# State space scan: running sums spread over the partitions by transfers, one subtraction per step, weight sums three loads behind

## The chip, the cores and the metric

The kernel runs on one core of a Trainium2 chip. The metric is the device time of one execution in microseconds (us). A core has a matrix engine, TensorE (PE), with its weight loader (PEld), three elementwise engines, VectorE (DVE), ScalarE (ACT) and GpSimd (POOL), SyncE (SP), which here only issues transfers, and 16 DMA engines that move data between the device memory and the on-chip memory SBUF. Products land in PSUM, a second on-chip memory of eight banks.

## What is computed

The reference is a decoder trunk of two layers for 1024 tokens of width 1024. Layer 0 has a state space part and a gated short convolution side by side; layer 1 has attention over a sliding window. Each is followed by a norm, a gated feed-forward part and a gate of its own. The change touches the state space part and some sums that a later norm needs. The state space part has 16 heads of 64 channels in two groups and works in chunks of 128 tokens:

```python
a_cs = jnp.cumsum(da, axis=2)
seg = a_cs[:, :, :, None] - a_cs[:, :, None, :]
decay_ls = jnp.exp(jnp.where(causal, seg, -jnp.inf))
cb = jnp.einsum('bclgn,bcsgn->bclsg', cm, bm)
y_diag = jnp.einsum('bclsgr,bcsgrp->bclgrp', cb[..., None] * decay_ls, xdt)
...
y_off = jnp.einsum('bclgn,bcgrpn->bclgrp', cm, h_in) * jnp.exp(a_cs)[..., None]
y = y_diag + y_off + xs * d_skip
```

`a_cs` is the running sum of a head's decays within a chunk. For each head and chunk, a 128 x 128 mask holds the exponential of the difference of two of its values, for every pair of tokens.

## The kernel before

Activations lie with features on the partitions and tokens along the row. The large products are of fp32 numbers that are split in a high and a low part, so that one tile takes three products (L134, L135, L136). A weight unit of 128 x 1024 comes by `unit()` (L118 to L131): SP issues the load of `st` (L128), ACT rounds it to the high part (L129), and DVE or POOL makes the low part (L130, on POOL alone while the scan and the short convolution run). There are two `st` buffers and three of weights. The order of the instructions on each engine is set by a scheduler from the program and from priorities, of which the units have a high one; so products that belong to later columns stand between the instructions of the scan.

`steps()` (L813 to L890) makes the decays of all heads. `acs` has the running sums with tokens on the partitions. `A2` has them with heads on the partitions and tokens along the row, as a rounded value on partitions 0 to 15 (L888) and the rest on 32 to 47 (L889). `SEL`, a table of ones and zeros that is loaded (L825) and cast, picks heads out of `A2` in a product.

`ssd(g)` (L911 to L986) is the scan of head group g. It runs over Q = 0 to 3, quarters of 256 tokens, and in each over p = 0 to 3, pairs of heads. A quarter begins with the work per chunk: transposes `xst` (L925), `xdt` (L930), the products `cb` (L932) with their causal mask `cbm` (L933), `xw`, `bt`, `btok` and the states `st` and `h` (L936 to L949). Then a step for each pair, 32 in all for both groups:

- two products with `SEL` (L957) put the running sums of the two heads on all 128 partitions, in a PSUM bank (`seg`);
- four instructions on DVE (L964), one per head and chunk, subtract the partition's own running sum and take the minimum with 0, into `m`;
- ACT takes the exponential (L966), DVE multiplies by `cbm` (L967);
- four products make `yd` (L972), up to two make `yo` (L978), and a third product with `SEL` (L980) puts the running sums beside `yo`, by channel;
- ACT takes their exponential `e` (L982), and three DVE instructions join all to y (L145, L985, L986).

The convolution of the columns x, B and C that precedes the scan takes, per half of a column, one ACT instruction (L902), three multiply-adds on DVE, a Tanh on ACT (L907) and one more on DVE; L145 is the line of a helper that all of these multiply-adds share.

Behind the scan come eight columns of the short convolution, three times 24 products for each half of the tokens. The first of the three is copied by ACT as `c` (L1034). Between them runs `centres()` (L1005 to L1020): 44 loads of 512 KB into `dc`, issued by POOL (L1013) into a pool of two buffers, and for each a sum on ACT (L1017) one load behind.

Of the kernel before, what the change touches and what calls it, by code (L numbers as in the profile page):

```python
# [7 lines left out]
F32 = mybir.dt.float32  # L8
F32R = mybir.dt.float32r
AF = mybir.ActivationFunctionType  # L10
ALU = mybir.AluOpType
# [31 lines left out]
def trunk(ctx: ExitStack, tc: tile.TileContext, xT, pT, w_in, w_dt, w_out, w_q, w_k, w_v, w_o, w_gate, w_up, w_down,  # L43
# [25 lines left out]
    def pool(stack, name, bufs=1, side=None):  # L69
        return stack.enter_context(tc.tile_pool(name=name, bufs=bufs, side=side, reuse_waits="tile"))  # L70

    def bank(tag, name):
        if "ps8" in room:
            return room["ps8"][1].tile([P, HB], F32, tag="ps", name=name, bufs=8)
        return room["ps"][1].tile([P, HB], F32, tag=tag, name=name, bufs={"g": 2, "c": 1, "a": 3, "b": 2}[tag])
# [19 lines left out]
    def hs(H):  # L95
        return slice(H * HB, (H + 1) * HB)

    def f4(pool, name, tag="f"):
        return (pool or room["r"][1]).tile([P, NT], F32, tag=tag, name=name)
# [695 lines left out]
    with ExitStack() as mctx:  # L795
# [10 lines left out]

        cwh = ts.tile([P, 60], F32, name="cwh")
        V.tensor_scalar_mul(out=cwh, in0=vec[:, VC["conv_w"]:VC["conv_w"] + 60], scalar1=0.5)
        SEL = ts.tile([P, 8, P], F32R, name="SEL")
        A2 = ts.tile([P, NT], F32R, name="A2")  # L810
        V.memset(A2[:48].bitcast(F32), 0.0)

        def steps():  # L813

            nc.sync.dma_start(cst, consts)
            A.activation(mean, ones, AF.Copy, scale=1.0 / 1024.0)
            A.activation(mean_r, ones, AF.Copy, scale=1.0 / 512.0)
            nc.sync.dma_start(row, rows.broadcast_to([P, NROW]))
            wst = ts.tile([P, KT, 16], F32, name="wst")
            nc.sync.dma_start(wst, w_dt)  # L820
            Wdt = ts.tile([P, KT, 32], F32R, name="Wdt")
            A.copy(Wdt[:, :, 0:16], wst)
            G.tensor_sub(Wdt[:, :, 16:32], wst, Wdt[:, :, 0:16].bitcast(F32))
            sst = f4(prep, "pre").rearrange("p (a b) -> p a b", b=P)
            nc.sync.dma_start(sst[:48], sel)  # L825
            A.copy(SEL[:48], sst[:48])
            dtT = [ts.tile([32, HB], F32, name="dtT", tag="h", bufs=3) for _ in range(2)]
            for H in range(2):
                ps = gps("dt")
                for i in range(KT):  # L830
                    T.matmul(ps[:32], Wdt[:, i, :], X[i][H][:, 0, :], start=i == 0, stop=False)
                    T.matmul(ps[:16], Wdt[:, i, 0:16], X[i][H][:, 1, :], start=False, stop=i == KT - 1)
                A.copy(dtT[H], ps[:32])
            dps = bank("b", "dtt")
            for c in range(NCH):
                T.transpose(dps[:, c * 32:(c + 1) * 32], dtT[c // 4][:, (c % 4) * P:(c % 4 + 1) * P], ident[:32, :32])

            def sm(name):
                return ts.tile([P, P], F32, name=name)

            def smt(name):
                return ts.tile([P, P], F32, tag="smt", name=name, bufs=4)

            def c16(ap):
                return ap.rearrange("p (c h) -> p c h", h=16)

            def b16(ap):
                return ap.unsqueeze(1).broadcast_to([P, 8, 16])

            dt, acs, dx, cd = sm("dt"), sm("acs"), sm("dx"), sm("cd")  # L850
            xr = smt("xr")
            dv = dps[:, :256].rearrange("p (c l h) -> p c l h", l=2, h=16)
            V.tensor_tensor(out=c16(xr), in0=dv[:, :, 0, :], in1=b16(row[:, 0:16]), op=ALU.add)
            V.tensor_tensor(out=c16(xr), in0=c16(xr), in1=dv[:, :, 1, :], op=ALU.add)
            e = smt("e")
            stt(e, xr, -1.0, xr, ALU.mult, ALU.max)
            A.activation(e, e, AF.Exp, scale=-1.0)
            sden = smt("sden")
            V.tensor_scalar_add(out=sden, in0=e, scalar1=2.0)
            V.reciprocal(out=sden, in_=sden)  # L860
            V.tensor_tensor(out=e, in0=e, in1=sden, op=ALU.mult)
            V.tensor_tensor(out=sden, in0=e, in1=e, op=ALU.mult)
            pol = smt("pol")
            V.tensor_scalar_mul(out=pol, in0=sden, scalar1=1.0 / 17.0)
            for k in (15, 13, 11, 9, 7, 5, 3):
                stt(pol, pol, 1.0 / k, sden, ALU.add, ALU.mult)
            stt(pol, pol, 1.0, e, ALU.add, ALU.mult)
            V.tensor_scalar_max(out=xr, in0=xr, scalar1=0.0)
            stt(dt, pol, 2.0, xr, ALU.mult, ALU.add)
            ea = ts.tile([P, 16], F32, name="ea")  # L870
            A.activation(ea, row[:, 16:32], AF.Exp)
            da = smt("da")
            stt(c16(da), c16(dt), -1.0, b16(ea), ALU.mult, ALU.mult)
            cps = bank("a", "acs")
            T.matmul(cps[:, :P], tri, da, start=True, stop=True)
            V.tensor_copy(acs, cps[:, :P])
            tps = bank("a", "tot")
            T.matmul(tps[:, :P], ones, da, start=True, stop=True)
            A.activation(cd, tps[:, :P], AF.Exp)
            V.tensor_tensor(out=dx, in0=tps[:, :P], in1=acs, op=ALU.subtract)  # L880
            A.activation(dx, dx, AF.Exp)
            V.tensor_tensor(out=dx, in0=dx, in1=dt, op=ALU.mult)
            for H in range(2):
                ps = bank("a", "acst")
                for cc in range(4):
                    c = 4 * H + cc
                    T.matmul(ps[:16, cc * P:(cc + 1) * P], da[:, c * 16:(c + 1) * 16], tri, start=True, stop=True)
                A.copy(A2[0:16, hs(H)], ps[:16])  # L888
                V.tensor_sub(A2[32:48, hs(H)], ps[:16], A2[0:16, hs(H)].bitcast(F32))  # L889
            return dt, acs, dx, cd  # L890

        BC = {}
# [18 lines left out]
        def ssd(g):  # L911
# [3 lines left out]
            for Q in range(4):  # L915
# [35 lines left out]
                qs = slice(Q * 256, (Q + 1) * 256)  # L951
                for p in range(4):
                    j = 4 * g + p
                    gp = bank("a", "seg")
                    for k in range(2):
                        hd = 8 * g + 2 * p + k
                        T.matmul(gp[:, k * 256:(k + 1) * 256], SEL[:48, j, 64 * k:64 * k + 1].broadcast_to([48, P]), A2[:48, qs],  # L957
                                 start=True, stop=True)
                    M = ts.tile([P, HB], F32, tag="m", name="m", bufs=3)
                    for k in range(2):  # L960
                        for ci in range(2):
                            a = (2 * Q + ci) * 16 + 8 * g + 2 * p + k
                            o = slice(k * 256 + ci * P, k * 256 + (ci + 1) * P)
                            V.tensor_scalar(out=M[:, o], in0=gp[:, o], scalar1=acs[:, a:a + 1], scalar2=0.0,  # L964
                                            op0=ALU.subtract, op1=ALU.min)
                    A.activation(M, M, AF.Exp)  # L966
                    V.tensor_tensor(out=M.rearrange("p (k q) -> p k q", k=2), in0=M.rearrange("p (k q) -> p k q", k=2),  # L967
                                    in1=cbm.rearrange("p c l -> p (c l)").unsqueeze(1).broadcast_to([P, 2, 256]), op=ALU.mult)
                    yd = bank("a", "yd")
# [6 lines left out]
                    for ci in range(2):  # L976
                        if hin[ci] is not None:
                            T.matmul(yo[:, ci * P:(ci + 1) * P], hin[ci][:, p * P:(p + 1) * P],  # L978
                                     Ct_[:, (2 * Q + ci) * P:(2 * Q + ci + 1) * P], start=True, stop=True)
                    T.matmul(yo[:, 256:512], SEL[:48, j, :], A2[:48, qs], start=True, stop=True)  # L980
                    e2 = ts.tile([P, 256], F32, tag="e2", name="e2", bufs=2)
                    A.activation(e2, yo[:, 256:512], AF.Exp)  # L982
                    y = YS[j][:, qs]
                    stt(y, y, vcol("ssd_d", j), yd[:, 0:256], ALU.mult, ALU.add)
                    V.tensor_tensor(out=e2[:, lo:], in0=e2[:, lo:], in1=yo[:, lo:256], op=ALU.mult)  # L985
# [17 lines left out]
        cctx = ExitStack()  # L1003

        def centres():  # L1005
            cp = pool(cctx, "cen", bufs=2, side="right")
            units = [(l, f) for l in range(2) for f in range(NFF)]
            ts_ = {}
            for i in range(len(units) + 1):
                if i < len(units):  # L1010
                    l, f = units[i]
                    ts_[i] = cp.tile([P, KT, P], F32, tag="c", name="dc")
                    nc.gpsimd.dma_start(ts_[i], w_down[l, f])  # L1013
                if i >= 1:
                    l, f = units[i - 1]
                    t = ts_.pop(i - 1)
                    A.activation(t, t, AF.Identity, scale=-1.0 / 1024.0, accum_out=cen[:, l, f:f + 1])  # L1017
                    if f % 2 and f > 1:
                        V.tensor_add(cen[:, l, NFF + f // 2 - 1:NFF + f // 2], cen[:, l, f - 1:f], cen[:, l, f:f + 1])
                    yield  # L1020
# [338 lines left out]
```

## Time and profile before

| | |
|---|---|
| median of 3 runs | 2711.0 us (2708.25 to 2713.06) |
| profiled execution | 2714.06 us, of which the span 2712.2 us |
| mean granted clock of TensorE | 0.991 |
| PE busy | 2636.0 us, 97% of the span, 12234 instructions |
| DVE busy | 1761.5 us, 65%, 2691 instructions |
| ACT busy | 1133.7 us, 42%, 1824 instructions |
| POOL busy | 496.9 us, 18%, 431 instructions |
| bytes moved | 315.40 MB, mean 116 GB/s |
| scan of group 0 | about 91 to 222 us |
| scan of group 1 | about 222 to 326 us |
| rest of the short convolution, weight sums | about 326 to 456 us |

The span is the time from the first to the last instruction of the profiled execution; the little that is left of its time lies around it. Busy is the time in which an engine executes at least one instruction; matrix products are pipelined, so one lasts longer than the distance to the next. Rows of single lines give busy time, the mean duration of one, and the idle time of the engine just ahead of them with what ended it.

### The profile page before, as it was taken

How to read it: one execution, taken by the hardware profiler on the slowest of the kernel's cores; microseconds unless marked ns; L12 is line 12 of the kernel's file. 1: busy time of each engine (PE TensorE's matmuls, PEld its weight loads, DVE VectorE, ACT ScalarE, POOL GpSimd, SP SyncE). 2: the span in 40 equal slices, each digit the busy share in tenths (PEclk: the TensorE clock that was granted, in tenths of full speed). 3: DMA queues.
4: the chain of work that ended last, by engine and by line, in shares of the span. 5: the costliest groups of instructions: out<-in, count | busy, mean ns of one | idle time of the engine just before them, and what ended most of it. 6: DMA issues, size and time to landing. Idle time of an engine off the chain costs nothing.

```text
span 2712.2 us, 31793 instructions
## 1 busy us (share of the span) xinstructions
PE 2636.0 (97%) x12234; PEld 2128.4 (78%) x12234; DVE 1761.5 (65%) x2691; ACT 1133.7 (42%) x1824; POOL 496.9 (18%) x431
## 2 busy tenths in 40 slices
PE   8999999999998999999999999999989999999998
PEld 6777777887876888888887887778778888888877
DVE  6787512265578656667966637775975666589663
ACT  5442254142234333335446446674533333354461
POOL 1111133111213201202103321001240021021132
PEclk9999999999998999999999999999999999999999
DMA  3100164311113424538623420003233344485142
GB/s 137 39 24 32 57 231 171 114 49 43 59 43 124 152 88 149 181 119 294 231 88 138 134 70 25 16 17 109 93 116 109 117 171 157 150 311 189 47 170 86
DMA packets 112728, 315.40 MB, mean 116 GB/s; under 512 B 10768, under 2 KB 27536, under 8 KB 112576
## 3 DMA queue, kind: packets, MB, share of 16 engines
q1 hardware_dynamic: 76624, 184.37, 19.6%
q0 software_dynamic: 35952, 128.99, 13.5%
q8 instruction: 96, 1.57, 0.2%
q14 instruction: 56, 0.46, 0.1%
HBM read 240.97 MB, written 72.35 MB: 116 GB/s over the span
## 4 chain that ended last, share of the span: by engine, by line
PE 82%; DVE 9%; issue 4%; ACT 2%; POOL 1%; DMA 1%; SPq 0%; POOLq 0%; ACTq 0%; DVEq 0%
PE px L358 16%; PE g L135 8%; PE g L136 8%; PE g L134 8%; PE dx L619 8%; PE pz L358 8%; PE pg L721 5%; PE dy L619 5%; PE py L358 4%; PE o L1186 2%; DVE x L112 1%; PE pt L1177 1%; DVE lnq L182 1%; PE yd L972 1%; PE yo L978 1%
## 5 line engine op out<-in xcount | busy, mean ns | idle before, releaser
L134 PE MATMUL g<-x,W 128*128 128x512 f32 x992 | 399.5, 403 | 11.9 <-ACT W L129 4.9
L135 PE MATMUL g<-x,W 128*128 128x512 f32 x992 | 397.6, 401 | 4.6 <-DVE x L112 3.0
L136 PE MATMUL g<-x,W 128*128 128x512 f32 x992 | 397.4, 401 | 2.4 <-POOL W L130 2.4
L130 POOL TENSOR_TENSOR W<-st,W 128x1024 fp32r<-128x1024 f32 x63 | 153.0, 2429 | 798.8 <-ACT W L129 798.6
L134 PEld LDWEIGHTS g<-x,W 128*128 128x128 f32 x992 | 189.7, 191 | 56.1 <-ACT x L111 5.2
L358 PE MATMUL px<-T,wV 128*128 128x512 f32 x960 | 231.0, 389 | 1.2 <-DVE c L368 1.2
L135 PEld LDWEIGHTS g<-x,W 128*128 128x128 f32 x992 | 189.7, 191 | 49.7 <-DVE x L112 6.4
L136 PEld LDWEIGHTS g<-x,W 128*128 128x128 f32 x992 | 189.5, 191 | 43.8 <-POOL W L130 3.3
L619 PE MATMUL dx<-tt,wd 128*128 128x512 f32 x960 | 219.2, 389 | 0.0
L358 PEld LDWEIGHTS px<-T,wV 128*128 128x128 f32 x960 | 179.9, 188 | 39.8 <-DVE c L368 2.5
L619 PEld LDWEIGHTS dx<-tt,wd 128*128 128x128 f32 x960 | 180.2, 188 | 37.4
L129 ACT CAST W<-st 128x1024 fp32r<-128x1024 f32 (+1 forms) x101 | 104.6, 1039 | 197.3 <-PE g L136 133.4
L619 PE MATMUL dy<-tt,wd 128*128 128x512 f32 x720 | 171.1, 397 | 8.8 <-DVE tt L478 6.9
L619 PEld LDWEIGHTS dy<-tt,wd 128*128 128x128 f32 x720 | 137.1, 191 | 40.8 <-DVE tt L478 8.3
L721 PE MATMUL pg<-x,W 128*128 128x512 f32 (+1 forms) x600 | 133.9, 383 | 2.9 <-DVE x L112 2.3
L358 PE MATMUL px<-T,wS 128*128 128x512 f32 x480 | 118.3, 396 | 13.8 <-ACT c L368 13.8
L721 PEld LDWEIGHTS pg<-x,W 128*128 128x128 f32 x600 | 109.4, 188 | 26.3 <-DVE x L112 3.1
L358 PEld LDWEIGHTS px<-T,wS 128*128 128x128 f32 x480 | 92.0, 192 | 33.9 <-ACT c L368 14.6
L478 DVE TENSOR_TENSOR tt<-tf,tt 128x1024 fp32r<-128x1024 f32 x74 | 97.3, 1320 | 30.6 <-ACT tt L477 23.9
L358 PE MATMUL px<-x,wA 128*128 128x512 f32 x480 | 116.2, 391 | 0.0
L358 PE MATMUL pz<-T,wU 128*128 128x512 f32 x480 | 115.3, 389 | 0.0
L358 PE MATMUL py<-x,wA 128*128 128x512 f32 x480 | 115.3, 389 | 0.0
(317 smaller groups left out, 5257.5 us busy)
## 6 DMA issues: line engine op xcount, KB each, us to landing
tf<-hT POOLq DMA_DIRECT2D x70, 512.0 KB, 4.8
dc<-in_w_down POOLq DMA_DIRECT2D x44, 512.0 KB, 3.8
st<-in_w_gate SPq DMA_DIRECT2D x44, 512.0 KB, 3.2
st<-in_w_up SPq DMA_DIRECT2D x44, 512.0 KB, 4.0
st<-in_w_in SPq DMA_DIRECT2D x43, 512.0 KB, 3.3
hT<-n SPq DMA_DIRECT2D x40, 512.0 KB, 6.5
xsum<-xs POOLq DMA_DIRECT2D x32, 512.0 KB, 3.6
wr<-in_w_down SPq DMA_DIRECT2D x24, 512.0 KB, 6.1
```

The costliest lines, as they stand in the source:

```text
L112: (lo_eng or V).tensor_sub(X[:, 1, :], src, X[:, 0, :].bitcast(F32))
L129: A.copy(W[:, 0, ks], st[:, ks])
L130: lo_eng[k % len(lo_eng)].tensor_sub(W[:, 1, ks], st[:, ks], W[:, 0, ks].bitcast(F32))
L134: T.matmul(ps, W[:, 0, i, :], X[:, 0, :], start=first, stop=False)
L135: T.matmul(ps, W[:, 0, i, :], X[:, 1, :], start=False, stop=False)
L136: T.matmul(ps, W[:, 1, i, :], X[:, 0, :], start=False, stop=last)
L182: V.tensor_add(self.q[H], self.q[H], sq)
L358: T.matmul(ps, W[:, l, o + k, :], x[:, xl, :], start=first and k == 0 and j == 0, stop=k == 3 and j == 2, skip_group_check=True)
L478: V.tensor_sub(t[:, :, 1], st, t[:, :, 0].bitcast(F32))
L619: T.matmul(bs[p], W[:, l, 4 * i + p, :], tt[:, i, xl, :], start=fresh and kk == 0 and j == 0, stop=kk == n - 1 and j == 2, skip_group_chec ...
L721: T.matmul(ps[:, c:c + n], W[m][l][:, i, :], X[i][H][:, xl, c:c + n], start=i == j == 0, stop=i == KT - 1 and j == 2)
L1186: T.matmul(ov[64 * hd:64 * hd + 64, bi * P:(bi + 1) * P], vt[:, b - 1 + kb, vc], pt[hd][:, 2 * bi + kb, :], start=kb == kbs[0], stop=kb == 1)
```

## The change

The running sums with heads on partitions go to a small table in device memory, `acr`, in two halves: ACT copies them from PSUM to `at`, and SP issues the transfer. `A2`, `SEL`, its load and its cast are gone. For each step, SP issues one transfer that reads two rows of `acr` and writes them to all 128 partitions of an SBUF tile `seg` (256 KB, four buffers). One DVE instruction of 128 x 512 subtracts the partition's own sums, both inputs now in SBUF. The minimum moves to ACT: `Relu` of the negative, then the exponential of its negative. The exponential `e` is taken from `seg` in two halves of the partitions instead of from the third product. The pool of `dc` has four buffers, and the sum runs three loads behind.

```diff
-        SEL = ts.tile([P, 8, P], F32R, name="SEL")
-        A2 = ts.tile([P, NT], F32R, name="A2")
-        V.memset(A2[:48].bitcast(F32), 0.0)
+        acr = tc.dram_tile([16, NT], F32, name="acr")
...
-            sst = f4(prep, "pre").rearrange("p (a b) -> p a b", b=P)
-            nc.sync.dma_start(sst[:48], sel)
-            A.copy(SEL[:48], sst[:48])
...
-                A.copy(A2[0:16, hs(H)], ps[:16])
-                V.tensor_sub(A2[32:48, hs(H)], ps[:16], A2[0:16, hs(H)].bitcast(F32))
+                at = ts.tile([16, HB], F32, name="at", tag="at")
+                A.copy(at, ps[:16])
+                nc.sync.dma_start(acr[:, hs(H)], at)
...
-                    gp = bank("a", "seg")
-                    for k in range(2):
-                        hd = 8 * g + 2 * p + k
-                        T.matmul(gp[:, k * 256:(k + 1) * 256], SEL[:48, j, 64 * k:64 * k + 1].broadcast_to([48, P]), A2[:48, qs],
-                                 start=True, stop=True)
+                    gp = ts.tile([P, HB], F32, tag="seg", name="seg", bufs=4)
+                    nc.sync.dma_start(gp.rearrange("p (k q) -> p k q", k=2),
+                                      acr[2 * j:2 * j + 2, qs].unsqueeze(0).broadcast_to([P, 2, 256]))
                     M = ts.tile([P, HB], F32, tag="m", name="m", bufs=3)
-                    for k in range(2):
-                        for ci in range(2):
-                            a = (2 * Q + ci) * 16 + 8 * g + 2 * p + k
-                            o = slice(k * 256 + ci * P, k * 256 + (ci + 1) * P)
-                            V.tensor_scalar(out=M[:, o], in0=gp[:, o], scalar1=acs[:, a:a + 1], scalar2=0.0,
-                                            op0=ALU.subtract, op1=ALU.min)
-                    A.activation(M, M, AF.Exp)
+                    hd = 8 * g + 2 * p
+                    own = acs.rearrange("p (c h) -> p h c", h=16)[:, hd:hd + 2, 2 * Q:2 * Q + 2]
+                    V.tensor_tensor(out=M.rearrange("p (k c q) -> p k c q", k=2, c=2),
+                                    in0=gp.rearrange("p (k c q) -> p k c q", k=2, c=2),
+                                    in1=own.unsqueeze(3).broadcast_to([P, 2, 2, P]), op=ALU.subtract)
+                    A.activation(M, M, AF.Relu, scale=-1.0)
+                    A.activation(M, M, AF.Exp, scale=-1.0)
...
-                    T.matmul(yo[:, 256:512], SEL[:48, j, :], A2[:48, qs], start=True, stop=True)
                     e2 = ts.tile([P, 256], F32, tag="e2", name="e2", bufs=2)
-                    A.activation(e2, yo[:, 256:512], AF.Exp)
+                    for k in range(2):
+                        half = slice(64 * k, 64 * k + 64)
+                        A.activation(e2[half], gp[half, k * 256:(k + 1) * 256], AF.Exp)
...
-            cp = pool(cctx, "cen", bufs=2, side="right")
+            cp = pool(cctx, "cen", bufs=4, side="right")
...
-            for i in range(len(units) + 1):
+            for i in range(len(units) + 3):
...
-                if i >= 1:
-                    l, f = units[i - 1]
-                    t = ts_.pop(i - 1)
+                if i >= 3:
+                    l, f = units[i - 3]
+                    t = ts_.pop(i - 3)
```

The scheduler puts the instructions in another order with this. On PE, in the scan of group 0, a step stood alone among ordinary products (`g`) before. `A` is the table A2, `h` the state, and the number behind x is how many rows alike follow each other:

```order
L972 MATMUL yd<-m,xdt 64x128 x4
L978 MATMUL yo<-xbc_663,h 128x128 x2
L980 MATMUL yo<-A_187,SEL 128x256
L957 MATMUL seg<-A_187,SEL 128x256 x2
L134 MATMUL g<-x_133,W 128x512
L135 MATMUL g<-x_133,W 128x512
L136 MATMUL g<-x_133,W 128x512
```

With the change, in the second quarter of the same group, the `yd` and `yo` of three steps follow each other, with only the transposes `xst` of the next quarter between them:

```order
L938 MATMUL st<-xw,btok 128x512
L966 MATMUL yd<-m,xdt 64x128 x4
L972 MATMUL yo<-xbc_660,h 128x128 x2
L966 MATMUL yd<-m,xdt 64x128 x4
L921 MATMUL xst<-cst,xbc_189 128x128
L921 MATMUL xst<-cst,xbc_190 128x128
L921 MATMUL xst<-cst,xbc_329 128x128
L972 MATMUL yo<-xbc_660,h 128x128 x2
L966 MATMUL yd<-m,xdt 64x128 x4
L972 MATMUL yo<-xbc_660,h 128x128 x2
```

From the first `xst` to the last `yd` of group 0 there are 321 ordinary products before and 165 with the change; in group 1, 278 and 150. Between the groups there are now 123 in a row.

On SP the queue held nothing but weight loads in the scans, behind the load of SEL. With the change the loads of `seg` stand among them:

```order
L128 DMA st<-in_w_in 128x1024 x5
L885 DMA acr<-at 16x512
L951 DMA seg<-acr 128x2x256
L885 DMA acr<-at 16x512
L951 DMA seg<-acr 128x2x256 x3
L128 DMA st<-in_w_in 128x1024
L951 DMA seg<-acr 128x2x256 x2
L128 DMA st<-in_w_in 128x1024 x2
L951 DMA seg<-acr 128x2x256 x4
```

All 32 loads of `seg` stand ahead of the last 23 weight loads of this part.

On ACT, in the short convolution, this stood between two copies of `c` before, eight sums (`dc`) in all:

```order
L1034 COPY c<-g 128x512
L1017 ACTIVATE dc,vec<-dc 128x1024 x3
L1042 ACTIVATE ysc_2829<-spre,vec 128x512
L1017 ACTIVATE dc,vec<-dc 128x1024 x5
L129 CAST W<-st 128x1024
L1034 COPY c<-g 128x512
```

With the change it is eleven, and all 44 are done some columns earlier:

```order
L1029 COPY c<-g 128x512
L1012 ACTIVATE dc,vec<-dc 128x1024 x4
L1037 ACTIVATE ysc_2524<-spre,vec 128x512
L1012 ACTIVATE dc,vec<-dc 128x1024 x7
L129 CAST W<-st 128x1024
L1029 COPY c<-g 128x512
```

Behind the short convolution, the rows of every engine are the same in both.

## Rows read from the trace of the kernel before

**Rows 1.** Busy time by stretch; last columns granted clock, DMA share, GB/s.

```profile
91.00:222.00 131.00, 125.37 (x657) 92.73 (x656) 112.56 (x228) 51.84 (x91) 17.56 (x7) 1.00 0.08 29
222.00:326.00 104.00, 101.35 (x551) 75.85 (x550) 73.62 (x167) 27.78 (x50) 14.24 (x6) 1.00 0.09 31
326.00:456.00 130.00, 123.91 (x530) 101.01 (x529) 28.32 (x50) 68.27 (x113) 46.81 (x54) 0.97 0.62 215
...
420.00:432.00 12.00, 8.03 (x29) 5.92 (x28) 2.92 (x4) 7.96 (x13) 6.84 (x6) 0.86 0.72 260
```

**Rows 2.** Groups by line on PE, 91 to 326 us.

```profile
L972 PE MATMUL yd<-m,xdt 128*64 128x128 f32 x256 | 21.3, 284 | 7.2 <-DVE m L967 7.2
...
L957 PE MATMUL seg<-A,SEL 48*128 48x256 f32 x64 | 12.6, 277 | 0.0
L980 PE MATMUL yo<-A,SEL 48*128 48x256 f32 x32 | 12.2, 381 | 0.0
```

**Rows 3.** Timeline of PE, an undisturbed run of products (start, duration, line).

```profile
326.12 0.39 PE L135 MATMUL g<-x,W 128*128 128x512 f32 x1
...
335.89 0.39 PE L136 MATMUL g<-x,W 128*128 128x512 f32 x1
```

**Rows 4.** Timeline of PE at the end of one step.

```profile
146.42 0.38 PE L980 MATMUL yo<-A,SEL 48*128 48x256 f32 x1
146.64 0.39 PE L957 MATMUL seg<-A,SEL 48*128 48x256 f32 x2
146.96 0.50 PE L136 MATMUL g<-x,W 128*128 128x512 f32 x1
```

**Rows 5.** Groups by line on DVE, 91 to 326 us.

```profile
L964 DVE TENSOR_SCALAR m<-seg,acs 128x128 f32<-128x128 f32 x128 | 39.5, 345 | 5.0 <-PE seg L957 5.0
L145 DVE SCALAR_TENSOR_TENSOR xbc<-pre,cwh,xbc 128x512 f32<-128x512 f32 (+3 forms) x39 | 34.2, 881 | 2.0 <-ACT xbc L902 1.6
...
L145 DVE SCALAR_TENSOR_TENSOR xbc<-th,xbc 128x512 f32<-128x512 f32 x14 | 9.6, 683 | 0.8 <-ACT th L907 0.8
```

**Rows 6.** One line's instructions, L967: ns least/middle/most.

```profile
L967 DVE TENSOR_TENSOR m<-m,cbm x32: 679/691/2437, 101.6 to 322.1; 128x512 f32<-128x512 f32 x32
```

**Rows 7.** Groups by line on ACT, 91 to 326 us.

```profile
L966 ACT ACTIVATE m<-m 128x512 f32<-128x512 f32 x32 | 20.2, 631 | 45.4 <-DVE m L964 45.4
...
L982 ACT ACTIVATE e<-yo 128x256 f32<-128x256 f32 x32 | 12.3, 384 | 66.7 <-PE yo L980 66.7
```

**Rows 8.** DMA issues, with KB each and us to landing.

```profile
hC<-sg SPq DMA_DIRECT2D x8, 256.0 KB, 2.2
```

**Rows 9.** Timeline of DVE at the end of the decays.

```profile
66.89 0.68 DVE L889 TENSOR_TENSOR A<-acst,A 16x512 fp32r<-16x512 f32 x1
71.84 3.24 DVE L145 SCALAR_TENSOR_TENSOR xbc<-pre,cwh,xbc 128x512 f32<-128x512 f32 x3 [4.28 <-ACT xbc L902]
```

**Rows 10.** Waits of PE, 326 to 456 us: total, times, longest.

```profile
PE g L134 <- ACT c L1034: 3.6, 2, 2.7
PE g L136 <- POOL W L130: 2.4, 2, 1.2
```

**Rows 11.** Timeline of ACT among the weight sums.

```profile
414.97 1.06 ACT L1017 ACTIVATE dc<-dc 128x1024 f32<-128x1024 f32 x1 [1.49 <-DMA dc<-in_w_down]
...
422.33 1.06 ACT L1017 ACTIVATE dc<-dc 128x1024 f32<-128x1024 f32 x1 [1.26 <-DMA dc<-in_w_down]
```

**Rows 12.** Busy time by stretch, a stretch with heavy transfers elsewhere.

```profile
1260.00:1270.00 10.00, 10.00 (x46) 8.28 (x45) 7.29 (x8) 4.62 (x8) 3.93 (x6) 1.00 1.05 403
```

**Rows 13.** Timeline of POOL and DVE around one low part.

```profile
150.05 2.39 POOL L130 TENSOR_TENSOR W<-st,W 128x1024 fp32r<-128x1024 f32 x1 [17.41 <-ACT W L129]
...
151.02 1.97 DVE L967 TENSOR_TENSOR m<-m,cbm 128x512 f32<-128x512 f32 x1 [1.37 <-ACT m L966]
```

**Rows 14.** One tile's instructions, seg: ns least/middle/most.

```profile
L964 DVE TENSOR_SCALAR m<-seg,acs x128: 336/346/352, 93.2 to 321.0; 128x128 f32<-128x128 f32 x128
```

**Rows 15.** Groups by line on POOL, 91 to 326 us.

```profile
L130 POOL TENSOR_TENSOR W<-st,W 128x1024 fp32r<-128x1024 f32 x13 | 31.8, 2446 | 204.2 <-ACT W L129 204.2
```

## The prediction

> **What bounds the kernel now.** I read the table by stretches first, then the lines of each engine in them, then single timelines where a number needed a place. The order of the instructions shows that behind the short convolution every engine runs the same rows in the same order before and after. So only three stretches can change: scan of head group 0 (91 to 222 us), scan of group 1 (222 to 326 us) and the short convolution with the weight sums (326 to 456 us). In all three TensorE (PE) is the bound, with little idle time: 131.00 - 125.37 = 5.6 us in the first, 104.00 - 101.35 = 2.7 us in the second, 8.3 us together [rows 1]. VectorE (DVE) is next, 112.56 and 73.62 us. Nearly all of the scans' PE idle time is one wait: yd for the mask product of L967, 7.2 us [rows 2]. In the third stretch PE runs 530 products, and an undisturbed product takes 0.227 us (43 of them from 326.12 to 335.89 us) [rows 3]; 530 x 0.227 = 120.3 of 130 us, so 9.7 us are lost there.
>
> **The change part by part.**
>
> *SEL products leave PE.* Each of the 32 steps gives up three: L980 at 146.42 and two of L957 at 146.64, with the next ordinary product at 146.96 [rows 4]. That is 0.54 us a step, 32 x 0.54 = **17.3 us**. The busy sums of the two lines, 12.6 + 12.2 = 24.8 us [rows 2], overlap their neighbours and are the outer bound. PE is the engine waited for here, so I take the whole 17.3 us off the path.
>
> *One subtraction for four.* DVE loses 128 instructions that keep it busy 39.5 us [rows 5] and gains 32 of 128x512. The nearest row to the new one is the product of L967, the same engine, size and kind with both inputs in SBUF: 0.69 us in the middle [rows 6]. 32 x 0.69 = 22.1 us, 17.4 us less. The bounds are 0.68 us, the smallest of L967, and its largest, 2.44 us; the latter is a rival below.
>
> *Minimum on ACT.* A Relu of 128x512 should cost what the exponential of L966 does, 0.63 us; e2 becomes two instructions on half the partitions, at most 0.38 us each as the whole one has now [rows 7]. ACT gains 32 x (0.63 + 0.38) = 32.3 us at most. It was busy 51.84 + 27.78 = 79.6 of 235 us [rows 1], so its total is no bound; it lengthens the way from subtraction to product, which is the rival on the slower side.
>
> *Products moved.* Between the first transpose and the last yd of group 0 stood 321 ordinary products, now 165; in group 1, 278 and now 150. The 156 and 128 that left (35.4 and 29.1 us) run unmixed between the groups and behind them at the same 0.227 us: no cost by themselves. But they were what PE did while DVE worked. For group 0 PE now has 125.37 - 8.6 - 35.4 = 81.4 us. On DVE the convolution that follows 24 products, (34.2 + 9.6) / 13 = 3.37 us [rows 5], goes along: 156 / 24 x 3.37 = 21.9 us. DVE keeps 112.56 - 19.8 + 11.0 - 21.9 = 81.9 us. For group 1 PE has 101.35 - 8.6 - 29.1 = 63.6 us and DVE at most 73.62 - 19.8 + 11.0 = 64.8 us. The engines come out level, where DVE had 13 and 28 us of slack. Level engines that hand each step back and forth wait more: I let PE's waits double, 8.3 to 16.3 us, **+8.0 us**. The ends are no growth and 1 us a step more, both rivals below. The moved convolutions, 21.9 us of DVE, lie beside 123 products (28 us) between the groups and are covered; were that cover gone, the start of group 1 would wait for its B and C, and some of the 8 us is for this.
>
> *Transfers.* 34 new ones stand on SP's queue: 2 of acr, 32 of seg at 256 KB. DMA is 8 to 9% busy in the scans [rows 1], and a load of that size lands in 2.2 us [rows 8]. The first subtraction follows a write and a load: from 66.89 us, when the running sums are ready now, 2 x 2.2 us makes 71.3, and DVE sat idle until 71.84 anyway [rows 9]. With four buffers later ones are issued four steps ahead; a step takes 4 us or more (63.6 / 16), the load 2.2. Weight loads stand in the same queue and wait for POOL's low parts, so a seg load can be queued behind one. Its four buffers cover some 12 us of that. I cost it at nothing; if the cover goes, the subtraction is late. The removed SEL load, its cast, the zeroing of A2 and the two A2 differences lie ahead of the first step, in that idle time: nothing.
>
> *Weight sums three behind.* PE's two waits here are for the copy c, 3.6 us, and for a weight's low part on POOL, 2.4 us [rows 10]; what is left of the 9.7 us is lower clock, as in 420 to 432 us, where the granted clock was 0.86 after such a gap [rows 1]. The copy is late since it is queued on ACT behind sums, which run one per 2.45 us (three from 414.97 to 422.33 us) though one lasts 1.06: each waits for its load [rows 11]. Two buffers let one load be under way while one is read; four let three. ACT's order now has 10, 8, 11 and 8 sums between copies of c, which are 72 products or 16.3 us apart, and all 44 are done earlier. With 1.5 weight units beside them, 11 sums ask for 12.5 x 0.524 MB = 6.55 MB in 16.3 us, 402 GB/s; the mean, 8.8 sums, 331 GB/s. The trace reached 260 GB/s at a DMA share of 0.72 here, 361 at full share, and 403 GB/s in another stretch [rows 1, 12]. I take 361: the stretch of 11 lasts 18.1 us, 1.8 over; the others fit. So 9.7 becomes 1.8, **-7.9 us**. Ends: nothing left (-9.7), or the rate stays at 260 GB/s (a rival).
>
> *The sum.* -17.3 + 8.0 - 7.9 = -17.2 us. The profiled execution took 2714.06 us, 2712.2 of span and 1.9 around it; it becomes 2696.9. It stands 3.1 us over the median of 2711.0, so against the median: **2694 us**. A measurement can tell about 0.2%, 5.4 us, from no change: faster means under 2705.6, slower over 2716.4.
>
> **The rivals.**
>
> *A. Waits don't grow.* The orders put three steps' yd and yo back to back, with the masks of several steps made ahead; DVE has 17.4 us less to do. For it: over 32 steps yd waits only 7.2 us now [rows 2], some of it where POOL had held DVE (rival C). Against: the levelled loads. -17.3 - 7.9 = -25.2: **2686 us**.
>
> *B. The loads stay the bound of the sums.* At 260 GB/s the 44 sums and 7.5 units of five stretches take 51.5 x 0.524 / 0.260 = 104 us against 5 x 16.3 = 82: 22 us lost instead of 9.7, since the order now packs them into fewer products. -17.3 + 8.0 + 12.4 = +3.1: 2714 us; midway to the forecast, some 300 GB/s, **2703 us**. Against: the 260 came with at most two sums' loads under way, and 403 GB/s has been seen.
>
> *C. POOL holds the new subtractions.* At 150.05 POOL began a low part of 2.39 us; the L967 begun at 151.02 took 1.97 us, and ended 0.55 us behind it [rows 13]. L967 ranged from 679 to 2437 ns [rows 6], while no L964, whose tile comes from PSUM, took over 352 [rows 14]. The new subtraction reads both tiles from SBUF, as L967 does, so 32 more instructions can be held. At worst each of POOL's 13 products [rows 15] holds one on the path for 2.44 - 0.69 = 1.75 us: 22.8 us of waits beside the 8.3, in place of my 8.0. -17.3 + 22.8 - 7.9 = -2.4: **2709 us**. Against: DVE has many two-input instructions already, and a product can hold but one at a time; and fewer products fall into the scans now. The Trainium skill has this as a rule (SBUF — State Buffer, "Who interferes with whom"): a VectorE instruction with two SBUF inputs and a GpSimd instruction that reads SBUF share one port, and whichever has it keeps the other out for its whole length. The trace agrees as far as these rows go; by the rule this part of the change speaks against it, and the sum would be C's.
>
> *D. The chain from subtraction to product.* Per step it now holds two ACT passes where there was one, and each needs DVE before and behind it. ACT already stood idle 45.4 us until L964 was done [rows 7]. If the level engines lose 1.3 us a step (Relu and exponential, 2 x 0.63) where neither can go ahead, waits rise by 32 x 1.3 = 41.6 us: -17.3 + 41.6 - 7.9 = +16.4: **2727 us**. It decides once the growth passes 17.3 + 7.9 + 5.4 = 30.6 us, about 1 us a step. Against: three mask buffers, and orders that start subtractions ahead of the products of earlier steps.
>
> **How the numbers follow.** My forecast 0.42 (2687 to 2702 by its ends), A 0.18, B 0.15, C 0.12, D 0.13. Faster takes 0.41 of the forecast, A, 0.10 of B and 0.05 of C: 0.74. Same takes 0.01 of the forecast, 0.05 of B, 0.05 of C and 0.01 of D: 0.12. Slower takes 0.12 of D and 0.02 of C: 0.14. The range runs from below A, with nothing left in the sums' stretch as well, to past C: 2681 to 2712 us, leaving out D, B's far end and a little of C, 2 in 10.
>
> **What would show it.** Right: PE's idle time in the two scans together 12 to 20 us with no wait for a seg load; sums at 1.2 to 1.5 us each and one short wait for c; the third stretch ending about 17 us earlier. Wrong: yd waiting some 1 us at most steps (D); subtractions over 2 us beside POOL's products (C); sums still 2 us apart and c waiting 3 us or more with the clock falling behind it (B); waits as now (A). A subtraction that waits for a transfer would overturn the term I set to nothing.

## The result, and the profile after

The changed kernel took 2679.4 us in the median of 4 runs (2678.2 to 2684.2), beside 2712.0 us for the kernel before: a ratio of 0.988, with a 95% interval of 0.986 to 0.990, 32.6 us less. On a second chip, later, it was 2680.6 beside 2717.2 us (0.987, 0.985 to 0.988). Faster was the likeliest side in the prediction, but 2679.4 lies below its range (2681 to 2712), and the gain is nearly twice the 17.2 us of the sum.

The stretches of [rows 1] end earlier now. In the table by stretch, with the same columns as there, the scans are 88 to 162 and 190 to 262 us, with unmixed products between them (row left out), and the last row is the stretch of the weight sums:

```profile
88.00:162.00 74.00, 71.13 (x416) 52.32 (x414) 67.19 (x126) 44.44 (x86) 9.58 (x4) 0.98 0.26 79
...
190.00:262.00 72.00, 68.84 (x407) 50.31 (x406) 63.85 (x124) 37.46 (x74) 7.85 (x4) 0.98 0.21 66
262.00:353.00 91.00, 90.97 (x402) 75.00 (x401) 22.97 (x45) 61.82 (x105) 39.40 (x50) 1.00 0.80 289
```

PE (third column) is idle 2.9 and 3.2 us in the scans and not at all beside the sums. DVE (fifth) is busy 67.2 of 74.0 and 63.9 of 72.0 us: high, but not level with PE. From the 100th to the 1000th ordinary product, counted in PE's timeline, these are the whole rows of the kernel before and of the changed one; the stretch is 313.7 and 290.2 us long:

```profile
36.90:350.60 313.70, 305.41 (x1563) 229.90 (x1562) 225.60 (x461) 115.03 (x198) 46.30 (x26) 1.00 0.13 44
```

```profile
33.90:324.10 290.20, 284.17 (x1467) 218.30 (x1466) 208.08 (x371) 166.74 (x302) 56.49 (x48) 0.99 0.36 117
```

PE's waits in that stretch of the changed kernel (us in total, times, longest) answer to the 7.2 us of yd in [rows 2]. Together they are 5.8 us, against 8.3 before, and the two longest, 4.0 us, stand where each group starts and the first `cb` waits for the convolution of B and C:

```profile
PE cb L928 <- DVE xbc L145: 4.0, 2, 2.2
PE yd L966 <- DVE m L961: 1.4, 4, 0.5
PE yo L972 <- DVE xbc L145: 0.4, 1, 0.4
```

These two waits cost more than their length. Behind each, PE was granted 0.50 of its clock (1.2 of 2.4 GHz) for a while: from 90.8 to 94.2 us, with ordinary products 0.43 us apart instead of 0.227, and from 193.2 to 196.6 us. The first of the two, in the timeline (start, duration, line) and in the table by stretch, where the clock is the third value from the right:

```profile
90.33 0.46 PE L928 MATMUL cb<-xbc,xbc 128*128 128x128 f32 x2 [1.84 <-DVE xbc L145]
```

```profile
90.80:94.20 3.40, 3.40 (x10) 2.52 (x10) 3.27 (x4) 1.16 (x3) 2.05 (x1) 0.50 0.08 29
```

PE was busy for 6.8 us at half clock, so about half of that, 3.4 us, was lost. The kernel before shows none of this between products 100 and 1000 in its profile.

The groups by line on ACT in the sums' stretch and the wait of a sum for its load (us, times) answer to [rows 11]. A sum waited for its load 21 times, 21.0 us in all, and no product waited for a copy of c (no wait of PE stands between 262 and 420 us):

```profile
L1012 ACT ACTIVATE dc<-dc 128x1024 f32<-128x1024 f32 x44 | 46.6, 1060 | 22.9 <-DMA dc<-in_w_down 21.0
```

Where the 36.0 us between the two profiled spans (2712.2 and 2676.2) went, by the times at which PE begins the same ordinary products:

| part | before | changed | difference |
|---|---|---|---|
| start to product 100 | 36.9 | 33.9 | -3.0 |
| product 100 to 1000 (scans) | 313.7 | 290.2 | -23.5 |
| product 1000 to 1600 (sums) | 146.2 | 136.4 | -9.8 |
| the rest | 2215.4 | 2215.7 | +0.3 |

The first row is chance. In the profile of before the products between 15 and 20 us stand 0.43 us apart, twice the 0.227 of later ones, and in that of the changed kernel they don't. But the other profiles that start as the changed kernel does came to product 100 at 34.5 to 36.7 us, and those that start as the kernel before does at 34.1 to 36.0. The medians of four runs each show 32.6 us, which agrees with the other rows.

### The profile page after: what moved, and what is told of

Read it like the earlier page. It is cut to its first block, busy times and chain, and to the rows that moved or that the text cites. A ratio compares the mean times of both kernels' runs of the same rounds, so it can differ in the third digit from the quotient of the medians.

```text
span 2676.2 us, 31658 instructions
## 1 busy us (share of the span) xinstructions
PE 2604.5 (97%) x12138; PEld 2109.7 (79%) x12138; DVE 1739.0 (65%) x2592; ACT 1162.6 (43%) x1887; POOL 496.1 (19%) x431
## 3 DMA queue, kind: packets, MB, share of 16 engines
q1 hardware_dynamic: 85328, 192.63, 20.8%
## 5 line engine op out<-in xcount | busy, mean ns | idle before, releaser
L134 PE MATMUL g<-x,W 128*128 128x512 f32 x992 | 396.2, 400 | 7.9 <-ACT W L129 5.3
L135 PE MATMUL g<-x,W 128*128 128x512 f32 x992 | 394.0, 397 | 8.9 <-DVE x L112 4.8
L136 PE MATMUL g<-x,W 128*128 128x512 f32 x992 | 392.4, 396 | 0.0
L135 PEld LDWEIGHTS g<-x,W 128*128 128x128 f32 x992 | 187.7, 189 | 53.8 <-DVE x L112 8.3
L134 PEld LDWEIGHTS g<-x,W 128*128 128x128 f32 x992 | 187.9, 190 | 50.0 <-ACT W L129 5.3
L136 PEld LDWEIGHTS g<-x,W 128*128 128x128 f32 x992 | 187.5, 189 | 39.0 <-issue 2.7
```

What stands on the lines that cost most here:

```text
L134: T.matmul(ps, W[:, 0, i, :], X[:, 0, :], start=first, stop=False)
L135: T.matmul(ps, W[:, 0, i, :], X[:, 1, :], start=False, stop=False)
L136: T.matmul(ps, W[:, 1, i, :], X[:, 0, :], start=False, stop=last)
```

## The experiments

All ran in five rounds beside the kernel before on the same chip; that kernel's median was 2715.5 us on the chip of the first four, 2717.2 on that of the next four and 2717.6 on that of the last. The changed kernel itself, run there too, is the base for the second four; beside the first four and the last four it was not run, and its time there is only known as its share of the kernel before (0.986 to 0.990 at first, 0.985 to 0.988 in this run):

> The changed kernel itself, as the base on this chip for the other three: 2679 us where the kernel before takes 2712, a ratio of 0.988. If its first 40 us come without the stretch at half the clock that the kernel before had there in its profiled run, that is seen here again; if it is chance, the first 100 ordinary products end at some 36 us instead of 34.

It came out at 0.987, with product 100 at 34.5 us, and with the same 290.3 us from product 100 to 1000.

**One part alone.** `scan_only` is the changed kernel with the sums as before, `sums_only` the reverse:

```diff
-            cp = pool(cctx, "cen", bufs=4, side="right")
+            cp = pool(cctx, "cen", bufs=2, side="right")
...
-            for i in range(len(units) + 3):
+            for i in range(len(units) + 1):
...
```

> The changed kernel with the weight sums as before (two buffers, one load behind). The forecast gave the scan -17.3 + 8.0 = -9.3 us: about 2702 us. The reading of the changed kernel's trace (a step's three SEL products cost 0.74 us with the changeover behind them, and PE's waits in the scans fell from 8.3 to 5.8 us) gives -20 to -26 us: about 2686 to 2692 us. If the sums made most of the gain, over 2705 us.

> The kernel before with the weight sums alone changed (four buffers, three loads behind). Forecast: -7.9 us, 2704 us, with one short wait for c left. Reading of the changed kernel's trace: the whole loss goes, -9.7 us, 2702 us, no wait of PE in that stretch and the clock at 1.00 there. Rival (loads bound at 260 GB/s): slower than before, 2720 us or more, with longer waits for c.

Measured: `scan_only` 2691.0 us, 0.991 (0.990 to 0.992), 24.5 us less; `sums_only` 2703.3 us, 0.996 (0.994 to 0.997), 12.2 us less. The scan gave more than twice the 9.3 us of the forecast, and the parts add up to the whole within what the runs can tell. In the stretch that lost 9.7 us before [rows 1], `sums_only` has PE busy all the time, at full clock:

```profile
326.00:456.00 130.00, 130.00 (x575) 107.67 (x574) 33.55 (x53) 70.56 (x116) 51.79 (x55) 1.00 0.61 222
```

With the sums put back, the two waits of [rows 10] are back in `scan_only`:

```profile
PE g L134 <- ACT c L1029: 4.0, 2, 3.4
PE g L136 <- POOL W L130: 2.0, 2, 1.2
```

**The price of the SEL products.** `dead_three` puts three idle products per step behind yo; what they write is read by nobody.

```diff
+T.matmul(yo[:, 256:512], mean_r[:48, :], X[0][0][:48, 0, 0:256], start=True, stop=True)   (three times)
                     e2 = ts.tile([P, 256], F32, tag="e2", name="e2", bufs=2)
```

> The changed kernel with three idle products of 48x128 and 256 columns per step put back behind yo, into columns that nobody reads; the rest of the computation is as it was. Forecast's price of 0.54 us a step: +17.3 us against the changed kernel, 2697 us. Price with the changeover, 0.74 us: +23.8 us, 2703 us. If PE is not the bound in the scans any more: under +6 us, below 2686 us.

Measured: 2706.5 us, 0.997 (0.996 to 0.998), 24 us over the changed kernel's share of the base (0.988 x 2715.5 = 2682). From product 100 to 1000 it took 311.0 us, 20.8 more, of which waits are 1.2: 19.6 us, 0.61 us a step. One of the two stretches at half clock did not come in this run, which hides 1.7 us: the products cost 21.3 us, 0.67 us a step. Either is between the two prices, and PE is the bound.

**More work on DVE.** `sub_twice` makes the subtraction twice; `four_sub` has the four instructions of before, reading SBUF, and no Relu.

```diff
-                    V.tensor_tensor(out=M..., in0=gp..., in1=own..., op=ALU.subtract)
+                    V.tensor_tensor(out=M..., in0=gp..., in1=own..., op=ALU.subtract); V.tensor_tensor(out=M..., in0=gp..., in1=own..., op=ALU.subtract)
```

> The changed kernel with each of the 32 subtractions made twice into the same tile: 22 us more on DVE, 11 a group. If the engines are as level as the forecast had them, nearly all of it shows: +15 to +22 us, 2694 to 2701 us. By the changed kernel's busy times (DVE 67 of 74 and 64 of 72 us) the slack of 7 and 8 us takes most: +3 to +10 us. If the order of the steps hides DVE altogether: under +3 us.

> The changed kernel with the four DVE instructions per step of before (subtract and minimum, 128x128, one input now in SBUF instead of PSUM), and so without the Relu on ACT. If they last 0.31 to 0.35 us as before, DVE gets 17 us more and ACT 20 us less. DVE on the path, as the doubled subtraction says: +12 to +17 us against the changed kernel. The transfers and products alone made the gain: under +4 us. If one input in SBUF makes the four quicker than 0.2 us each, DVE has less to do than with one subtraction: 0 to -3 us.

Measured: `sub_twice` 2703.8 us, 0.996 (0.994 to 0.997), 21 us over the changed kernel's share; `four_sub` 2699.7 us, 0.994 (0.993 to 0.996), 19 us over the changed kernel. From product 100 to 1000 they took 310.1 and 304.6 us, 19.9 and 14.4 more. PE's waits rose from 5.8 to 20.1 us in `sub_twice`. These are the longest, all on DVE:

```profile
PE cb L928 <- DVE xbc L145: 4.9, 2, 2.7
PE cb L928 <- DVE h L945: 4.5, 3, 1.7
PE yd L966 <- DVE m L961: 4.3, 3, 2.0
```

So the 15 us by which DVE's busy time falls short of the two scans' length are no slack: of 22 us more on DVE, 19.9 showed, 14.3 as waits and the rest in the main as half clock behind them. The scans of the changed kernel stand at the edge where DVE sets the time. Each of the four instructions took 0.28 us in `four_sub` (0.35 from PSUM in [rows 14]). They kept DVE busy for 35.0 us, 12 more than the 23.0 of one subtraction, and taking 20 us of Relu from ACT did not help: a little more than the first expectation, DVE on the path.

**Less work on DVE in the kernel before.** `one_sub` has before's kernel with one subtraction from PSUM and the Relu on ACT.

> The kernel before with one subtraction and the Relu on ACT instead of the four DVE instructions; the SEL products, the transfers and the weight sums stay as before. DVE gets 17 us less, PE's own work is untouched. If DVE's relief by itself makes part of the gain, PE's waits in the scans (8.3 us) shrink and it is 2 to 6 us faster than the kernel before. If DVE had slack there as the busy times of before say (112.6 of 131 and 73.6 of 104 us): within 2 us of it.

Measured: 2719.5 us, 1.001 (1.000 to 1.002). PE's waits in the scans went from 8.3 to 5.7 us, and the stretch from product 100 to 1000 from 313.7 to 310.8, but PE's waits for c rose to 8.7 us from the 3.6 of [rows 10]. The stretch from product 1000 to 1600 took 6.6 us more (152.8 us). DVE's relief alone gains nothing that lasts; whether the 2.9 us of the scans would stay with the sums three loads behind, no run shows. Beside `four_sub` it says that the single subtraction with its Relu is worth little while the SEL products keep PE busy, and 14 us of the stretch once they are gone.

**The chain over ACT.** `relu_twice` makes the Relu twice.

```diff
-                    A.activation(M, M, AF.Relu, scale=-1.0)
+                    A.activation(M, M, AF.Relu, scale=-1.0); A.activation(M, M, AF.Relu)
```

> The changed kernel with the Relu made twice in each step (the second changes nothing): 0.63 us more in the chain from subtraction to mask product, 20 us more on ACT. Rival D of the prediction (the chain of two engines sets the step): +15 to +20 us. By the busy times of ACT in the two scans of the changed kernel (44 of 74 and 37 of 72 us) and the masks made ahead: under +4 us.

Measured: 2687.3 us, 0.989 (0.988 to 0.991), 6.7 us over the changed kernel (the intervals just touch); 5.0 us of it lie between products 100 and 1000, with waits of 9.8 us. That is 0.2 us a step, neither expectation: masks made ahead cover most of the chain, not all.

**POOL's hold.** `low_dve` and `low_dve_before` make the low parts of the weights on DVE, in the changed kernel and in the one before. The line that is changed holds from the scan of group 0 to the end of the short convolution, so it reaches further than the scans of which the expectations speak.

```diff
         group(0)
-        lo_eng[:] = [G]
+        lo_eng[:] = [V]
```

> The changed kernel with the low parts of the weights made on DVE while the scans run, so that no POOL product runs beside DVE there. If POOL's hold of two-input instructions costs the scans much (rival C), faster by 5 us or more. By the changed kernel's trace (one subtraction of 2.3 us and one mask product of 2.9 us among 64, 3.8 us in all, and some 8 units at 1.2 us more on DVE): +3 to +10 us slower.

> The kernel before with the low parts of the weights on DVE while the scans run. If POOL's hold makes the waits of yd (rival C's mechanism: 7.2 us in the profile of before, mask products of up to 2.44 us), they go and it is 4 to 7 us faster. If they come from the order of the steps or from DVE's load (13 units at 1.2 us more): no faster, or up to 5 us slower.

Measured: `low_dve` 2675.1 us, 0.985 (0.984 to 0.987), 5.5 us under the changed kernel in the medians on that chip, with intervals that overlap (0.985 to 0.988 for the changed one), so that the times alone don't show it faster; `low_dve_before` 2710.3 us, 0.997 (0.996 to 0.998). In the scans of `low_dve_before` PE waited for nothing: 304.0 us from product 100 to 1000, 9.7 less than before. Part of it came back: the stretch from product 1000 to 1600 took 6.3 us more, and PE waited 11.0 us for c there. This is the line of L967 there (ns least/middle/most), whose row before ended at 2437 [rows 6]:

```profile
L967 DVE TENSOR_TENSOR m<-m,cbm x32: 678/686/695, 99.5 to 319.6; 128x512 f32<-128x512 f32 x32
```

No DVE instruction, the low parts of 1.22 us among them, lasted over 1.3 us in the scans of either. So the waits before were POOL's hold, though DVE took on 13 low parts. The order on PE is not quite the same in the two kernels, so the profile of before has to say it too, and does: four of the five waits of yd, 5.8 us, end with an L967 that lasted 1.97 to 2.44 us beside a low part, and the fifth and one wait of cb, 2.2 us, come behind multiply-adds of 2.02 and 2.85 us that were held. Only 0.3 us of the 8.3 is left without such a sign. The expectation for `low_dve` was wrong in sign: it counted 3.8 us of held subtractions and mask products and left out the convolution's multiply-adds. Of seven instructions in the changed kernel that lasted over 1.3 us between 85 and 330 us, six are on L145, 11.2 us over an undisturbed 0.69 in all seven, and the convolution is what cb waits for: 0.9 us in `low_dve`, 4.0 in the changed kernel. From product 100 to 1000 `low_dve` took 286.7 us, 3.5 less: 1.8 of waits and 1.7 of clock.

**Fewer buffers for seg.** `seg_two` has two instead of four.

> The changed kernel with two buffers for the spread running sums instead of four. The forecast has the loads hidden (2.2 us to land, a step of 4 us): with two buffers a load still has a step's time, under +3 us against the changed kernel. If the loads are late when they queue behind weight loads that wait for their low parts (up to 19 us on SP's queue): +5 us or more, with DVE waiting for seg at several steps.

Measured: 2685.4 us, 0.989 (0.987 to 0.990): 5 us over the changed kernel's median on the second chip, with intervals that overlap. The stretch is clearer: from product 100 to 1000 it took 5.1 us more, and PE's waits rose by 4.8 us, which is the second expectation. From the tile's own rows (idle time by releaser: us, times; then us to landing):

```profile
L956 DVE TENSOR_TENSOR m<-seg,acs x32: 676/683/2851, 69.2 to 263.1; 128x512 f32<-128x512 f32 x32
...
  DMA seg<-acr: 10.1, 6
...
DMA to landing us min/median/max: 3.1/3.5/4.7
```

With four buffers the same idle time is 5.1 us in three places, all ahead of the first yd. Four buffers hide the loads; two do not.

**The last addition on POOL.** `add_pool` is `low_dve` with the last addition of each step on POOL, which has nothing but a few loads to issue there.

```diff
-                    V.tensor_add(y[:, lo:], y[:, lo:], e2[:, lo:])
+                    G.tensor_add(y[:, lo:], y[:, lo:], e2[:, lo:])
```

> The changed kernel with the low parts on DVE (2675 us where the changed one took 2681) and the last addition of each step, y plus e, on POOL. DVE gets 12 us less. If DVE's load is what is left to gain and POOL does not disturb it: 1 to 4 us faster than with the low parts alone. If POOL's two-input additions hold DVE's two-input instructions for their length: no faster, up to 8 us slower, with subtractions and mask products stretched over 0.7 us.

Measured: 2675.3 us, 0.985 (0.983 to 0.986). It and `low_dve` have the lowest times of the study; by these they can't be told from each other, and hardly from the changed kernel, whose interval begins at 0.985. The stretch from product 100 to 1000 tells more: 283.9 us, against 286.7 for `low_dve` and 290.2 to 290.3 in three profiles of the changed kernel's scans (the third is `scan_only`). It has 2.7 us of waits and nothing at half clock. Both are single profiles. POOL's additions lasted 0.83 us and stretched the subtractions little (0.77 us in the mean, from 0.68, and up to 1.23).

## Why the prediction was right in its direction and wrong in its size

The stretch from product 100 to 1000 splits into PE's waits, 900 ordinary products at 0.227 us (204.3 us) and the remainder, which is the smaller products with the changeovers to and from them, and what is lost at half clock. The fourth column is PE's busy time where it was granted 0.50 of its clock, and the next one the remainder less half of that:

| run | stretch | PE's waits | remainder | PE busy at 0.50 | remainder at full clock | DVE busy |
|---|---|---|---|---|---|---|
| before | 313.7 | 8.3 | 101.1 | 0 | 101.1 | 225.6 |
| one_sub | 310.8 | 5.7 | 100.8 | 0 | 100.8 | 210.0 |
| low_dve_before | 304.0 | 0 | 99.7 | 0 | 99.7 | 229.7 |
| dead_three | 311.0 | 7.0 | 99.7 | 3.4 | 98.0 | 212.3 |
| changed | 290.2 | 5.8 | 80.1 | 6.8 | 76.7 | 208.1 |
| sub_twice | 310.1 | 20.1 | 85.7 | 16.8 | 77.3 | 231.4 |
| four_sub | 304.6 | 17.4 | 82.9 | 12.5 | 76.6 | 218.8 |
| relu_twice | 295.3 | 9.8 | 81.2 | 9.5 | 76.4 | 213.5 |
| seg_two | 295.3 | 10.6 | 80.4 | 6.3 | 77.3 | 213.3 |
| low_dve | 286.7 | 4.0 | 78.4 | 3.4 | 76.7 | 212.6 |
| add_pool | 283.9 | 2.7 | 76.9 | 0 | 76.9 | 207.9 |

At full clock the remainder has two levels only: 98.0 to 101.1 us with three more small products a step, 76.4 to 77.3 us without. So the 23.5 us that the scans gained are 24.4 us of products, 2.5 us of waits, less 3.4 us of clock. The forecast had 17.3 of products and 8.0 of growing waits, -9.3 in all.

- **SEL products leave PE: right, but too small.** The term was 17.3 us. The remainder fell by 21.0 us, and by 24.4 us at full clock, 0.76 us a step; 21.3 us, 0.67 a step, came back with `dead_three`. The step that failed is reading the price as the distance from L980's start to the next ordinary product, 0.54 us. It took for granted that an ordinary product behind yo would start when L980 did. In fact it starts earlier. These are the timelines of one step's end, before and then changed (start, duration, line):

```profile
145.78 0.71 PE L978 MATMUL yo<-xbc,h 128*128 128x128 f32 x4
...
147.30 0.40 PE L134 MATMUL g<-x,W 128*128 128x512 f32 x1
```

```profile
156.33 0.71 PE L972 MATMUL yo<-xbc,h 128*128 128x128 f32 x4
156.80 0.48 PE L136 MATMUL g<-x,W 128*128 128x512 f32 x1
157.11 0.39 PE L134 MATMUL g<-x,W 128*128 128x512 f32 x1
```

  From the first yo to the second ordinary product it is 147.30 - 145.78 = 1.52 us, and 157.11 - 156.33 = 0.78 us: 0.74 us less where ordinary products follow, close to the mean of 0.76. The outer bound, 24.8 us, just held it. How much of the 3.1 us between 24.4 and 21.3 is the place of the three products, and how much the changed order, no run separates.

- **Waits: wrong in sign, and as large a miss.** The forecast let them double, +8.0 us. They fell by 2.5, and with the 3.4 us of clock lost behind them PE is 0.9 us worse off. The step that failed is the working of the levelled engines under "Products moved": it gave DVE 81.9 and PE 81.4 us in group 0, where the profile has 67.2 and 71.1. It took the moved products and their convolutions out of a stretch of 131 us that also held 7.6 us behind group 0's last yd (214.4 us), with work of group 1 in it, which began at 202.2 us (the 278 products of group 1 are counted from group 0's last yd; from its own first transpose there are 311). And more of DVE's work left than it counted: 228 - 3 x 16 = 180 instructions were to become 154 without the convolutions, and are 126. Of the 28, 14 belong to the 7.6 us, 3 are subtractions made ahead of the scan, and most of the others are convolutions: 39 multiply-adds of L145 ahead of the Tanh became 13, 26 fewer, where the working took out 6.5 x 3. DVE was not level with PE, and the waits that it was to cause at every step did not come: yd waits 1.4 us in all. Of the 4.0 us at the group starts, 2.2 stand where group 1 waits for its B and C, for which the prediction kept some of its 8 us. That the idea behind the term was not idle is shown by `sub_twice`: 22 us more on DVE cost 19.9 us.
- **Where the 8.3 us of waits came from** was put down in the prediction to several things. `low_dve_before` and the profile of before show that nearly all of them were POOL's hold. So they were no measure of how closely PE and DVE stood, and doubling them had no ground. Rival C therefore had the mechanism right, and its price wrong: of the 32 new subtractions one was held (2.29 us, at 68 us, ahead of the first step), and the scans now hold 8 low parts instead of 13. The rule of the Trainium skill named there (SBUF — State Buffer, "Who interferes with whom") agrees with the runs that take POOL's products out of the scans: the longest L967 of `low_dve_before` lasted 0.695 us, where it had been 2.437.
- **Weight sums: right, a little small.** The term was -7.9 us; the stretch from product 1000 to 1600 lost 9.8 us and now takes 136.4 us, 600 x 0.227 = 136.2 and so nothing above its products. The 1.8 us kept for the place with eleven sums did not come, though that place was slower than forecast: from one copy of c to the next it took 21.4 us, where the working had 18.1, and no product waited for the copy. Here the step that failed is that a late copy costs PE its delay:

```profile
302.55 0.56 ACT L1029 COPY c<-g 128x512 f32<-128x512 f32 x1
...
323.94 0.58 ACT L1029 COPY c<-g 128x512 f32<-128x512 f32 x1
```

- **Transfers at nothing: right, by a cover that was needed.** A load of seg landed in 3.4 us, not 2.2, and the write of acr in 2.7. [rows 8] is a store; the loads of 256 KB in the same view of before (`st<-in_w_in`, 3.1 us) stood nearer. The first subtraction waited for its load until 68.15 us, ahead of the first yd at 100. `seg_two` shows that the two more buffers are worth 5 us.
- **Rivals.** A (waits don't grow, 2686 us) came nearest. B's price is excluded by `sums_only`, but its premise held in part: the loads still set the pace of the sums, which stood 1.97 us apart in the mean (44 from 267.3 to 351.8 us) where the forecast had 1.2 to 1.5, at 289 GB/s. D is excluded as it stood, 1.3 us a step; `relu_twice` puts the sensitivity at 0.2 us a step for 0.63 us more of chain.

What stays open is when the clock falls. Each stretch at half clock in the table begins beside one of PE's longer waits, but not each such wait has one: the two of 1.78 us in the kernel before had none, and in `sums_only`, with the same order on PE, one of 1.77 us had. So one such stretch more or less, 1.7 us, can be luck, though the changed kernel's scans lost the same 3.4 us in three profiles.

## What to carry to other kernels

Price a product that leaves a full engine by the whole run from the last instruction ahead of it to the second one behind it, in both kernels where the order is known, not by its own start and the next. When work moves out of a stretch, bound the stretch by the first and last instruction of the work itself; a few us of the neighbour's work in it turn slack into none. And before a wait is put down to an engine's load, look at the longest instances of the instruction that ends it: waits that a loaded engine seemed to cause went to zero here when another engine's long instructions were taken out, though the loaded one took on more. A wait of a full engine is priced with the clock that falls behind it: 4.0 us of waits came with 3.4 us more here.

## What the runs showed of the hardware that was not expected

An instruction of DVE with one tile input, in SBUF, was held too. In `four_sub` the 128x128 subtraction with minimum, whose other inputs are a column of one value per partition and a constant, took 0.27 to 0.28 us, but up to 2.48 us beside POOL's low parts (ns least/middle/most); from PSUM [rows 14] it never was:

```profile
L958 DVE TENSOR_SCALAR m<-seg,acs x128: 271/280/2477, 69.5 to 266.5; 128x128 f32<-128x128 f32 x128
```

The products of 256 columns on 48 partitions cost PE 0.67 to 0.76 us for three at full clock, changeovers included: as much as three ordinary ones of 512 columns on 128 partitions (3 x 0.227 = 0.68), or a little more.
